# Moving the first weight transfer of a two-layer transformer kernel to ScalarE's queue, merging three early transfers and cutting the last output scaling into four pieces

## The chip, the cores and the metric

The kernel runs on one core of a Trainium2 chip. A core has TensorE (PE, the matmul engine, with its weight loads listed as PEld), VectorE (DVE), ScalarE (ACT), GpSimd (POOL) and SyncE (SP, which here only issues DMA transfers), and 16 DMA engines. The metric is the device time of one execution in microseconds; lower is better. Durations and start times below come from one profiled execution, counted from the start of its span.

## The reference

The reference is a two-layer hybrid block over 16 meta tokens and 256 input tokens of width 1024. Cut to what matters here:

```
h = concat(meta, x)
for li in range(2):
    h = h + mixer(rms_norm(h, norm_mix_g[li]), w_in[li], ...)      # retention, HGRN2, differential attention
    h = h + conv_ffn(rms_norm(h, norm_ffn_g[li]), w_ffn_in[li], ...)
out = rms_norm(h, norm_final_g)[:, PAD:]                           # 256 x 1024
```

with rms_norm(x, g) = x * rsqrt(mean(x*x) + 1e-6) * g. All weights are float32, and most of the time goes into the products with them.

## The kernel before, in words

**Weights.** All weight matrices are laid out on the host as one stream of 128x128 tiles in the order of use, in chunks of eight tiles (`CHUNK_TILES`, 128x1024 float32, 512 KB). `_Weights.next` (class at L554) does for each chunk what a float32 product needs when it is made of three fast products: a DMA brings the chunk to `wraw`, ACT rounds it to `whi`, DVE computes the remainder `wlo = wraw - whi`. There are three `wraw` buffers and four each of `whi` and `wlo`. Chunks 0 and 1 are brought and split in two halves of four tiles, all others whole.

**Products.** `products` (L862 to L864) issues three matmuls for each weight tile: `whi` with the rounded activations `xh`, `whi` with their remainder `xl`, `wlo` with `xh`. Activations lie as features by tokens: 128 partitions by 272 tokens, eight feature tiles k.

**The start.** x (with the meta tokens) lies in `h`, eight feature tiles, brought in four transfers of two tiles. `Norm.take` makes `xh` (ACT) and `xl` (DVE) of a tile k. The first norm is handled in a late way: the products start from x scaled by the gain alone, and the factor 1/rms (`rstd`) is multiplied into the products. For `rstd`, ACT squares pairs of tiles (`sum`, then `two_c` three times), POOL adds them, DVE folds the two halves, PE sums over partitions with a ones matrix (`ms`), and ACT takes Ln and Exp. After the fourth pair of output columns (`DEFER`), x is scaled by `rstd` itself: POOL makes `y`, ACT and DVE make a new `xh` and `xl` of it, for eight k. The first two output groups (`hq` 0 and 1) run interleaved over k = 0 to 3, so that chunk 0 holds the tiles of k = 0 (its first half) and k = 1, chunk 1 those of k = 2 and 3. Chunk 2 holds k = 4 to 7 of the first group, chunk 3 those of the second. Then come `hf` 0 to 3, two chunks each; `hf` 2 is the first that reads the scaled x.

**What sets the order.** The program is recorded as a list of operations with an engine, an estimated cost and a key, the due time (`plan.key`); `_Plan.order` (L407) plays this list through with the costs and picks, whenever an engine is free, the operation that can start first, by key among equals. `issue` (L508) emits the instructions in that order, and each engine runs its own in that order. In it a DMA issued by SP is taken as complete 2.0 us after its cost, others at once.

**The end.** `final` (L1340) computes the last products with tokens on partitions, two blocks of 128 tokens by two halves of 512 columns, and then for each block: ACT squares and sums, DVE multiplies the first half by the final gain, ACT takes Ln and Exp for the factor `dm`, then DVE scales the second half (L1390, from PSUM, with gain) and ACT the first half (L1391), and SP and ACT issue one output transfer of 256 KB each.

Nearly every instruction other than the matmuls is recorded through one helper, so its line is L549 in the profile; instructions are told apart by tile names.

## Time and profile before

| What | Value |
|---|---|
| Runs | 1330.01, 1329.83 and 1330.66 us; median 1330.01 |
| Profiled execution | 1330.22 us, span 1328.4 us, granted clock 0.999 |
| PE busy | 1317.2 us (99%), 11862 matmuls |
| DVE busy | 962.0 us (72%) |
| ACT busy | 813.3 us (61%) |
| POOL busy | 83.6 us (6%) |
| DMA | 219.07 MB, mean 165 GB/s |
| PE waits named in the trace | xl 2.8 us (3 times), ones_d 1.0 us, wlo 0.6 us |

The profiled execution is 1.8 us longer than its span and 0.2 us above the median of the runs. A busy share of PE of 99% does not mean that PE runs at its peak everywhere: matmuls overlap, and a matmul's row begins where it begins and may hold a wait. In a stream without waits, matmuls of 272 columns begin 0.125 us after one another.

### The profile page before, as it was taken

To read this page: it belongs to the slowest core of one execution; us is meant where nothing else is said; L and a number is where in the kernel's file an instruction comes from. 1 tells how busy PE (TensorE), PEld (TensorE's weight loads), DVE (VectorE), ACT (ScalarE), POOL (GpSimd) and SP (SyncE) were. 2 spreads that over 40 slices of the span, in tenths; PEclk is the share of its full clock that TensorE was granted. 3 is DMA by queue.
4 is the path that set the end of the run, shared out by engine and by line. 5 is a ranking of instruction groups with operands and counts; after the bars stand their busy time and mean duration, and the time that the engine had idled before them with its cause. 6 is when DMAs were issued, how large, how long until landed. Compare 5 with 4: busy or idle time off the path is not lost.

```text
span 1328.4 us, 28916 instructions
## 1 busy us (share of the span) xinstructions
PE 1317.2 (99%) x11862; PEld 1288.8 (97%) x11862; DVE 962.0 (72%) x1630; ACT 813.3 (61%) x1372; POOL 83.6 (6%) x161
## 2 busy tenths in 40 slices
PE   9999999999999999999999999999999999999998
PEld 9999999999999999999999999999999999999986
DVE  7575777697576689886564757776985867898753
ACT  6747454746676567665446474557565775766643
POOL 5000000001010020000030000000011100200000
PEclk9999999999999999999999999999999999999999
DMA  7644543443544545555555445444445445465653
GB/s 270 193 142 153 167 161 128 143 143 128 179 139 159 175 159 175 182 170 187 177 173 179 158 157 163 160 136 144 141 153 175 141 160 198 138 208 189 199 184 109
DMA packets 60755, 219.07 MB, mean 165 GB/s; under 512 B 6864, under 2 KB 6992, under 8 KB 60624
## 3 DMA queue, kind: packets, MB, share of 16 engines
q1 hardware_dynamic: 60336, 216.71, 49.6%
q8 instruction: 93, 1.52, 0.5%
q10 hardware_dynamic: 288, 0.52, 0.1%
q14 instruction: 38, 0.31, 0.1%
HBM read 216.16 MB, written 1.05 MB: 164 GB/s over the span
## 4 chain that ended last, share of the span: by engine, by line
PE 94%; DVE 4%; issue 1%; ACT 0%; DMA 0%; SPq 0%; DVEq 0%
PE main L862 27%; PE main L864 27%; PE main L863 26%; PE fo L1372 2%; PE fo L1374 2%; PE fo L1373 2%; PE lev L1053 1%; DVE two_b L549 1%; PE ds L1237 1%; DVE wlo L549 1%; PE ms L549 1%; PE do L549 1%; PE ro L549 1%; PE ho L549 1%; PE vt L549 1%
## 5 line engine op out<-in xcount | busy, mean ns | idle before, releaser
L862 PE MATMUL main<-xh,whi 128*128 128x272 f32 (+1 forms) x2368 | 693.4, 293 | 0.3 <-issue 0.3
L864 PE MATMUL main<-xh,wlo 128*128 128x272 f32 (+1 forms) x2368 | 680.4, 287 | 0.7 <-DVE wlo L549 0.6
L863 PE MATMUL main<-xl,whi 128*128 128x272 f32 (+1 forms) x2368 | 671.7, 284 | 2.8 <-DVE xl L549 2.8
L549 DVE TENSOR_TENSOR wlo<-wraw,whi 128x1024 fp32r<-128x1024 f32 (+1 forms) x408 | 496.8, 1223 | 201.2 <-ACT whi L549 200.3
L549 ACT ACTIVATE whi<-wraw 128x1024 fp32r<-128x1024 f32 (+1 forms) x408 | 426.5, 1048 | 231.5 <-PE main L863 166.1
L863 PEld LDWEIGHTS main<-xl,whi 128*128 128x128 f32 x2368 | 448.9, 190 | 4.0 <-DVE xl L549 3.4
L862 PEld LDWEIGHTS main<-xh,whi 128*128 128x128 f32 x2368 | 445.6, 188 | 2.1 <-issue 0.4
L864 PEld LDWEIGHTS main<-xh,wlo 128*128 128x128 f32 x2368 | 444.6, 188 | 2.0 <-DVE wlo L549 2.0
L549 DVE SCALAR_TENSOR_TENSOR two_b<-main,small,two_b 128x256 f32<-128x256 f32 (+2 forms) x144 | 65.4, 487 | 29.1 <-ACT two_b L549 27.4
L549 ACT ACTIVATE two_b<-main,small 128x272 f32<-128x272 f32 (+1 forms) x72 | 37.3, 566 | 28.7 <-PE main L864 28.7
L549 POOL TENSOR_TENSOR y<-h,rstd 128x272 f32<-128x272 f32 x32 | 34.8, 1121 | 316.4 <-ACT rstd L549 316.4
L864 PE MATMUL main<-ghi,wlo 128*128 128x272 f32 x176 | 51.0, 290 | 0.0
L862 PE MATMUL main<-ghi,whi 128*128 128x272 f32 x176 | 50.9, 289 | 0.0
L863 PE MATMUL main<-glo,whi 128*128 128x272 f32 x176 | 50.2, 285 | 0.0
L549 ACT ACTIVATE vsrc<-main 128x544 f32<-128x544 f32 x24 | 15.0, 626 | 39.4 <-PE main L864 39.2
L862 PE MATMUL main<-b0hi,whi 128*128 128x272 f32 (+1 forms) x128 | 38.2, 298 | 0.0
L862 PE MATMUL main<-b1hi,whi 128*128 128x272 f32 (+1 forms) x128 | 38.1, 298 | 0.0
L864 PE MATMUL main<-yhi,wlo 128*128 128x272 f32 (+1 forms) x128 | 36.7, 286 | 0.0
L864 PE MATMUL main<-b2hi,wlo 128*128 128x272 f32 (+1 forms) x128 | 36.6, 286 | 0.0
L864 PE MATMUL main<-b1hi,wlo 128*128 128x272 f32 (+1 forms) x128 | 36.6, 286 | 0.0
L864 PE MATMUL main<-b0hi,wlo 128*128 128x272 f32 (+1 forms) x128 | 36.6, 286 | 0.0
L862 PE MATMUL main<-yhi,whi 128*128 128x272 f32 (+1 forms) x128 | 36.5, 285 | 0.0
(244 smaller groups left out, 1933.0 us busy)
## 6 DMA issues: line engine op xcount, KB each, us to landing
wraw<-in_w SPq DMA_DIRECT2D x402, 512.0 KB, 3.4
h<-in_h SPq DMA_DIRECT2D x4, 272.0 KB, 5.6
dec<-in_dec SPq DMA_DIRECT2D x2, 544.0 KB, 5.3
wraw<-in_w SPq DMA_DIRECT2D x4, 256.0 KB, 4.9
const<-in_const SPq DMA_DIRECT2D x1, 937.0 KB, 5.9
gain<-in_gl SPq DMA_DIRECT2D x1, 512.0 KB, 5.2
out<-y ACTq DMA_DIRECT2D x2, 256.0 KB, 2.8
out<-y SPq DMA_DIRECT2D x2, 256.0 KB, 2.7
```

What stands on the lines that cost most here:

```text
L549: self.plan.add(self.name, lambda: f(*args, **kw), cost, outs, ins, args[2] if method == "activation" else None)
L862: nc.tensor.matmul(o, wh, hi, start=first, stop=False)
L863: nc.tensor.matmul(o, wh, lo, start=False, stop=False)
L864: nc.tensor.matmul(o, wl, hi, start=False, stop=last)
L1053: nc.tensor.matmul(o, keys, x, start=True, stop=True)
L1237: nc.tensor.matmul(ss[m][:, at : at + nk], q[half, hd, q0 : q0 + P], k[half, hd, :nk], start=True, stop=True)
L1372: nc.tensor.matmul(o, gh, wh, start=False, stop=False)
L1373: nc.tensor.matmul(o, gl, wh, start=False, stop=False)
L1374: nc.tensor.matmul(o, gh, wl, start=False, stop=end)
```

## The change

There are six edits.

1. The first half of chunk 0 is brought by ACT's DMA queue instead of SP's, with key -9.6, so that it is ACT's first instruction. The table load, which was ACT's first, is put ahead of the first activation, behind this transfer.
2. The second half of chunk 0 stays on SP's queue; chunk 1 is brought whole, while both chunks are still split into whi and wlo by halves.
3. x comes in three transfers instead of four: tiles 0-1, 2-3, and 4-7 in one.
4. The keys of `take` go from 1.4k - 4.0 to 1.4k - 6.5, and the rounding of a small constant (`ones_h`) is queued behind the xl of k = 1.
5. The planner's costs: the lag of a DMA is now held with the operation, 2.0 us for SP and 2.0 us plus the time for its bytes for other queues; an issue on ACT's queue costs 0.42 us instead of 0.06 us.
6. For the last group of `final`, the scaling is made in four pieces of 256 columns: ACT the first, DVE the third, POOL the second, DVE the fourth, with four transfers of 128 KB, on ACT's, SP's, SP's and ACT's queue.

On each engine the instructions are in the order of before from about chunk 12 on, up to the last group. In the first 40 us these rows differ. ACT before and after (`whi0a` is the first half of chunk 0, `xh4` is k = 4, `sq` the squares in the order of pairs, `fh` and `fl` the xh and xl of the scaled x):

```
before: table, ones_h, xh0, xh1, whi0a, sq0, whi0b, xh2, xh3, whi1a, sq1, whi1b, xh4, xh5, whi2, xh6, xh7, sq2, whi3, whi4, sq3, hq, whi5, rstd, whi6, ...
after:  DMA w0a, table, whi0a, xh0, xh1, whi0b, xh2, xh3, ones_h, sq0, whi1a, whi1b, sq1, xh4, xh5, xh6, xh7, whi2, sq2, whi3, whi4, sq3, hq, whi5, whi6, rstd, ...
```

and DVE:

```
before: xl0, xl1, wlo0a, wlo0b, xl2, xl3, wlo1a, wlo1b, xl4, xl5, wlo2, xl6, xl7, wlo3, wlo4, sum, wlo5, hq, ...,
        wlo9, fl4, fl5, fl6, hf1, fl7, wlo10, wlo11, masks
after:  wlo0a, xl0, xl1, wlo0b, xl2, xl3, wlo1a, wlo1b, xl4, xl5, xl6, xl7, wlo2, wlo3, wlo4, sum, wlo5, wlo6, hq, ...,
        wlo9, (parameters), fl4, fl5, masks, hf1, wlo10, fl6, fl7, wlo11
```

SP's queue begins with small, h0-1, w0b, h2-3, w1, h4-7, w2, w3, w4, w5, w6 (before: small, h0-1, w0a, w0b, h2-3, w1a, w1b, h4-5, w2, h6-7, w3, w4, w5, a second part of small, w6). On PE only the matmul `ms` moves, two tiles forward, into chunk 3.

The diff:

```
--- before.py
+++ after.py
@@ -302,11 +302,11 @@
 
 
 class _Op:
-    __slots__ = ("engine", "run", "cost", "key", "func", "tiles", "need", "after", "ready")
+    __slots__ = ("engine", "run", "cost", "key", "func", "tiles", "need", "after", "ready", "lag")
 
     def __init__(self, engine, run, cost, key, func):
         self.engine, self.run, self.cost, self.key, self.func = engine, run, cost, key, func
-        self.tiles, self.need, self.after, self.ready = set(), 0, [], 0.0
+        self.tiles, self.need, self.after, self.ready, self.lag = set(), 0, [], 0.0, 0.0
 
 
 class _Plan:
@@ -489,7 +489,7 @@
                     f.remove(min(f))
             engines[e] = t + cost
             self.busy[e] += cost
-            done = t + cost + (2.0 if e == "sp" else 0.0)
+            done = t + cost + op.lag
             for n in op.tiles:
                 left[n] -= 1
                 if left[n] == 0:
@@ -506,7 +506,9 @@
         return out
 
     def issue(self):
-        order = [None] + self.order()
+        order = self.order()
+
+        order.insert(next(i for i, op in enumerate(order) if op is not None and op.func is not None), None)
         with self.tc.manual_schedule():
             for op in order:
                 if op is None:
@@ -546,7 +548,10 @@
                 cost = max(0.214 if args[1].shape[-1] > 32 else 0.07, 4 * n / 2400)
             elif method == "dma_start":
                 cost = self.fixed + self.each * n * outs[0].shape[0]
-            self.plan.add(self.name, lambda: f(*args, **kw), cost, outs, ins, args[2] if method == "activation" else None)
+            op = self.plan.add(self.name, lambda: f(*args, **kw), cost, outs, ins, args[2] if method == "activation" else None)
+            if method == "dma_start":
+
+                op.lag = 2.0 if self.name == "sp" else 2.0 + 4 / 360e3 * n * outs[0].shape[0]
 
         return call
 
@@ -555,9 +560,9 @@
 
 
 
-    def __init__(self, plan, pool, w, act, dve, sp):
+    def __init__(self, plan, pool, w, act, dve, sp, first):
         self.plan, self.pool, self.w = plan, pool, w
-        self.act, self.dve, self.sp = act, dve, sp
+        self.act, self.dve, self.sp, self.first = act, dve, sp, first
         self.used = 0
         self.places = _places()
 
@@ -575,13 +580,19 @@
             hi = self.plan.tile(self.pool, room, F32R, "whi", 4, f"whi{c}")
             lo = self.plan.tile(self.pool, room, F32R, "wlo", 4, f"wlo{c}")
             self.plan.key = due - LEAD
-            pieces = 1 if c > 1 else 2
-            for p in range(pieces):
-                n = CHUNK_TILES // pieces
-                cols = slice(p * n * P, (p + 1) * n * P)
-                self.sp.dma_start(raw[:, cols], self.w[c][:, cols])
-                for first, at, step, runs, each in _runs(self.places[c][p * n : (p + 1) * n]):
-                    src = raw[:, (p * n + first) * P : (p * n + first + runs * each) * P].rearrange("p (r x) -> p r x", r=runs)
+
+            half = CHUNK_TILES // 2
+            for first in range(0, CHUNK_TILES, half if c == 0 else CHUNK_TILES):
+                cols = slice(first * P, (first + half if c == 0 else CHUNK_TILES) * P)
+                queue = self.sp
+                if (c, first) == (0, 0):
+                    queue, self.plan.key = self.first, -9.6
+                queue.dma_start(raw[:, cols], self.w[c][:, cols])
+                self.plan.key = due - LEAD
+            n = half if c < 2 else CHUNK_TILES
+            for a in range(0, CHUNK_TILES, n):
+                for first, at, step, runs, each in _runs(self.places[c][a : a + n]):
+                    src = raw[:, (a + first) * P : (a + first + runs * each) * P].rearrange("p (r x) -> p r x", r=runs)
                     self.act.activation(self.part(hi, at, step, runs, each), src, AF.Copy)
                     self.dve.tensor_tensor(out=self.part(lo, at, step, runs, each), in0=src, in1=self.part(hi, at, step, runs, each).bitcast(F32), op=SUB)
             self.plan.key = due
@@ -612,7 +623,7 @@
     pe = _Engine(plan, nc.tensor, "pe", 0.0, 4 / 2400)
     pool = _Engine(plan, nc.gpsimd, "pool", 0.04, 0.85e-3)
     sync = _Engine(plan, nc.sync, "sp", 0.06, 4 / 360e3)
-    act_queue = _Engine(plan, nc.scalar, "act", 0.06, 0.0)
+    act_queue = _Engine(plan, nc.scalar, "act", 0.42, 0.0)
 
     cp = ctx.enter_context(tc.tile_pool(name="cp", bufs=1))
     wp = ctx.enter_context(tc.tile_pool(name="wp", bufs=3))
@@ -622,7 +633,7 @@
     mp = ctx.enter_context(tc.tile_pool(name="mp", bufs=2, space=PSUM))
     bp = ctx.enter_context(tc.tile_pool(name="bp", bufs=2, space=PSUM))
 
-    weights = _Weights(plan, wp, a["w"], act, dve, sync)
+    weights = _Weights(plan, wp, a["w"], act, dve, sync, act_queue)
     serial = [0]
 
     def new(pool_, shape, dt, tag, bufs, name):
@@ -675,9 +686,9 @@
     plan.key = -10.0
     sync.dma_start(small[:, :S_LB], a["small"][:, :S_LB])
     h = fixed([P, KD, T], "h")
-    for k in range(0, KD, 2):
+    for k, n in ((0, 2), (2, 2), (4, 4)):
         plan.key = -9.0 if k == 0 else 1.4 * k - 7.0
-        sync.dma_start(h[:, k : k + 2, :].rearrange("p a t -> p (a t)"), a["h"][:, k * T : (k + 2) * T])
+        sync.dma_start(h[:, k : k + n, :].rearrange("p a t -> p (a t)"), a["h"][:, k * T : (k + n) * T])
     plan.key = 7.0 + EARLY
     sync.dma_start(small[:, S_LB:], a["small"][:, S_LB:])
     plan.key = 12.0 + EARLY
@@ -713,6 +724,7 @@
         pe.matmul(warm[:, :P], ones_d, ones_d, start=True, stop=True)
     plan.key = -5.0
     ones_h = ones_round(1.0 / 128, "ones_h")
+    rounded = plan.ops[-1]
     eps = fixed([P, 1], "eps")
     pool.memset(eps, EPS)
     fmap = fixed([P, DEPTH], "fmap")
@@ -943,8 +955,10 @@
         if li == 0:
             norm = Norm(small[:, S_GM : S_GM + KD], adds=pool)
             for k in range(KD):
-                plan.key = 1.4 * k - 4.0
+                plan.key = 1.4 * k - 6.5
                 norm.take([k])
+                if k == 1:
+                    plan.queue(rounded, plan.ops[-1])
             for j in range(4):
                 plan.key = 1.0 + 2.5 * j
                 norm.square([2 * j, 2 * j + 1])
@@ -1387,11 +1401,24 @@
                     continue
                 act.activation(ms[3], ms[1], AF.Ln, scale=1.0 / D, bias=ms[2])
                 act.activation(ms[3], ms[3], AF.Exp, scale=-0.5)
-                stt(y[:, t, cols], o, ms[3], gain[:, cols], MUL, MUL)
-                act.activation(y[:, t, :BANK], y[:, t, :BANK], AF.Copy, scale=ms[3])
-                for c, queue in ((1, sync), (0, act_queue)):
-                    cols = slice(c * BANK, (c + 1) * BANK)
-                    queue.dma_start(a["out"][:, t * D + c * BANK : t * D + (c + 1) * BANK], y[:, t, cols])
+
+                def part(first, n, queue, engine):
+                    yt = y[:, t, first : first + n]
+                    if engine is dve:
+                        stt(yt, o[:, first - BANK : first - BANK + n], ms[3], gain[:, first : first + n], MUL, MUL)
+                    elif engine is act:
+                        act.activation(yt, yt, AF.Copy, scale=ms[3])
+                    else:
+                        pool.tensor_scalar(out=yt, in0=yt, scalar1=ms[3], scalar2=None, op0=MUL)
+                    queue.dma_start(a["out"][:, t * D + first : t * D + first + n], yt)
+
+                if (t, c) == groups[-1]:
+                    for i, x in enumerate(((0, BANK // 2, act_queue, act), (BANK, BANK // 2, sync, dve), (BANK // 2, BANK // 2, sync, pool), (BANK + BANK // 2, BANK // 2, act_queue, dve))):
+                        plan.key = clock[0] + 0.1 * i
+                        part(*x)
+                else:
+                    part(BANK, BANK, sync, dve)
+                    part(0, BANK, act_queue, act)
 
         for name, j in ORDER:
             if name == "+ret":
```

## The prediction

> **What bounds the kernel now.** I read the page first, for the shares and the chain that ended last, then the timeline of the first 40 us and of the last 6, where the change lies.
>
> ```profile
> span 1328.4 us, 28916 instructions
> PE 1317.2 (99%) x11862; PEld 1288.8 (97%) x11862; DVE 962.0 (72%) x1630; ACT 813.3 (61%) x1372; POOL 83.6 (6%) x161
> ...
> PE 94%; DVE 4%; issue 1%; ACT 0%; DMA 0%; SPq 0%; DVEq 0%
> ```
>
> PE sets the time: 94% of the last chain is its own. Outside the first 40 us and the end the order on every engine is unchanged, so what the change can move is the start (the wait before PE's first product, and PE's gaps there) and the tail behind PE's last product. 0.2% of this kernel, about what a measurement can tell from no change, is 2.66 us.
>
> ```profile
> 0.73 1.28 ACT L513 ACT_TABLE_LOAD   x1 [0.73 <-PEq L1561]
> ...
> 1.18 0.42 SPq L549 DMA_DIRECT2D h<-in_h  x1
> 1.65 0.90 SPq L549 DMA_DIRECT2D wraw<-in_w  x2
> ...
> 4.02 0.94 ACT L549 ACTIVATE xh<-h,small 128x272 fp32r<-128x272 f32 x2 [1.69 <-DMA h<-in_h]
> ...
> 5.06 0.63 ACT L549 ACTIVATE whi<-wraw 128x512 fp32r<-128x512 f32 x1
> ...
> 6.47 0.39 PE L864 MATMUL main<-xh,wlo 128*128 128x272 f32 x1 [0.21 <-DVE wlo L549]
> ...
> 7.93 0.93 ACT L549 ACTIVATE xh<-h,small 128x272 fp32r<-128x272 f32 x2 [0.91 <-DMA h<-in_h]
> ...
> 10.16 0.39 PE L864 MATMUL main<-xh,wlo 128*128 128x272 f32 x1 [0.21 <-DVE wlo L549]
> ...
> 10.48 1.43 DVE L549 TENSOR_TENSOR wlo<-wraw,whi 128x512 fp32r<-128x512 f32 x1 [0.37 <-ACT whi L549]
> ...
> 12.66 1.21 DVE L549 TENSOR_TENSOR wlo<-wraw,whi 128x1024 fp32r<-128x1024 f32 x1
> ...
> 13.93 0.39 PE L864 MATMUL main<-xh,wlo 128*128 128x272 f32 x1 [0.21 <-DVE wlo L549]
> ```
>
> The first product starts at 5.75 and PE then stops at the third (6.47), at 9.44 and 10.16 (chunk 1, k = 2), at 11.97 (k = 3) and at 13.93 (chunk 2): against the pitch of 0.125 us these starts and the slow one behind each lose 2.2 us by 16 us. All wait for ACT's and DVE's splitting. From the chain of waits:
>
> ```profile
> 34.85 1.13 DVE wlo L549
> 35.98 0.42 DVE xl L549
> 36.45 0.39 PE main L863
> ```
>
> PE stops once more, 35.24 to 36.45 (1.06 us lost), for the first xl of the scaled x with k = 4 (`fl4`). So the most that the start can give is 2.2 + 1.06 + about 1 us of earlier begin, 4.3 us.
>
> ```profile
> 1322.94 0.53 ACT L549 ACTIVATE dm<-dm 128x1 f32<-128x1 f32 x2
> 1323.51 0.72 ACT L549 ACTIVATE y<-y,dm 128x512 f32<-128x512 f32 x1
> 1323.51 0.75 DVE L549 SCALAR_TENSOR_TENSOR y<-fo,dm,gain 128x512 f32<-128x512 f32 x1 [1.46 <-ACT dm L549]
> 1324.26 0.36 ACTq L549 DMA_DIRECT2D out<-y  x1
> ```
>
> The tail: 6.4 us from PE's last product to the end, of which scaling takes 0.75, a transfer 2.7 to 2.8 from issue to landing, closing about 1.3.
>
> **The start, step by step.** I give each instruction the later of its engine's last end and its inputs' ends, with these rows: xh 0.51 us (0.43 to the next), xl 0.49 (0.41), whi of a half 0.63 (0.53), whole 1.05 (0.95), wlo of a half 0.69 (0.60), whole 1.21 (1.14), squares 0.64. The same walk over the kernel before gives 13.87 for 13.93 and 36.91 for 36.45, so it runs 0.46 late by then; this is taken off below.
>
> *First weights.* ACT issues its transfer at 0.73 instead of SP's 1.65. The table load moves back by an issue (0.36 to 0.41), to 2.4; it is hidden, as ACT waits for data until 4.02 anyway. The shortest h transfer landed 2.8 us after issue: 3.5 for w0a, 3.7 with x's first tiles beside it. x landed at 3.98; sharing delays it by between nothing and 0.7 (the 0.67 that eight packets of 84 ns take); I take 4.25. whi0a 3.75 to 4.36, wlo0a 4.40 to 5.08, xh0 4.29 to 4.80, xl0 5.00 to 5.49, PE's second product 5.54, its third 5.67: 0.8 us ahead of 6.47. If w0a gained nothing, whi0a would still go ahead of xh0, 0 to 0.4 later than now.
>
> *k = 2.* Fewer bytes stand before h2-3 (1.08 MB, not 1.34); at the 250 GB/s of the first 16 us that is 1 us, so it lands at 6.7 instead of 7.9 (bounds 6.2 and 7.9). ACT then has xh2, xh3, ones_h (0.31, moved here from 2.03 where it cost nothing), the squares and whi1a: 6.75 + 2 x 0.43 + 0.25 + 0.55 = 8.4 to 9.0. The whole w1 lands at about 8.2 (cumulative bytes as before: w1a and w1b by 9.1), no later than ACT is ready; if it comes at 9.0, all below is 0.65 later. wlo1a ends at 9.73, PE goes on at 9.78: 0.38 ahead.
>
> *k = 3.* whi1b follows whi1a, wlo1b ends at 10.33; the stop at 11.97 (0.3) goes. Lead 0.7.
>
> *Chunk 2: here the lead is lost.* x's last four tiles land at once, at about 9.8 (11.8 for the last before), and the new order puts four xh ahead of whi2 and four xl ahead of wlo2; before, two of each stood behind. ACT: 10.0 + 4 x 0.43 = 11.7, whi2 to 12.74. DVE: the first xl meets POOL's sum. The row at 10.48 shows what that costs: a wlo of 0.69 took 1.43 beside POOL's 1.36. xl4 starts at 11.40, four xl end at 13.13, wlo2 goes 13.05 to 14.27, and PE's first wlo of chunk 2 is at 14.32 instead of 13.93: 0.4 behind. With the 0.15 that PE loses before at 15.45 for xl6 and xl7, 0.25 behind.
>
> *The norm.* The second sum (1.36) and wlo3 come 14.2 to 16.6, the third sum ends at 17.8, DVE's fold at 19.2, `ms` at 19.9. But rstd now stands behind whi6 on ACT, and w6 is issued when wlo3 frees its buffer (16.6) and lands 3.4 later (the median), 20.0; whi6 ends at 21.04, rstd at 22.06 against 21.55. Behind it wait POOL's eight y.
>
> *The scaled x.* The parameters' first half moves ahead of wlo7, which frees ACT for whi9 earlier; fl4 comes at 35.3, and PE, arriving at 35.8, no longer stops there: 1.06 gained. Late next: fl6. DVE now runs masks (0.32), hf1 (0.71) and wlo10 (1.21) ahead of it: 36.12 + 0.3 + 0.65 + 1.13 = 38.20, done 38.70, where PE wants k = 6 at 37.3. It goes on at 38.75; before, the same product was at 38.06. That is 0.69 late, less the walk's 0.46: **0.2 us slower**. The sum is small because four gains (0.8, 0.3, 0.15, 1.06) end in DVE's queue, which is busy 22.0 of the 24 us from 16 to 40.
>
> Everything from the second landing on shifts one for one with h2-3 and w1, so the landing bounds (0.5 early, 1.2 late) are the start's: -0.3 to +1.4; without the 0.69 of fl6 (if wlo10 falls early) -0.9.
>
> **The tail.** ACT and DVE make 256 columns in 0.51 and 0.48 (0.72 and 0.75 less 256 times the slopes, 0.21 and 0.27), so the first two transfers are issued at 1324.04 instead of 1324.26 and 1324.28; DVE's second piece ends at 1324.40, ACT issues it at 1324.43. POOL has no row for a scaling of 256 columns: bounds 0.31 (memset of 256) and 1.06 (256/272 of y's mean of 1.12, contended); nearest is the copy of 128 columns, 0.36, which with its slope gives 0.56, and SP's first issue hides it until 1324.4. At 1.06 its transfer is issued 0.2 later. The four pieces start 0.22 earlier but are finer, and a packet of half the size takes more than half the time (1280 bytes 55 ns, 2048 bytes 84: 9% more over the 1.5 us of data). Gain 0.1; bounds 0.5 gained and 0.15 lost, the latter from two more landings for SP to await.
> The Trainium skill (DMA: Bandwidth & Descriptors, Anatomy of one DMA) puts about 2.0 us of fixed cost on each transfer plus bytes over 436 GB/s; by that, as an estimate, a 128 KB piece issued 0.15 later lands 0.15 earlier. The rows give 2.7 to 2.8 for 256 KB, near its 2.6.
>
> **Sum.** +0.2 - 0.1 = +0.1 us. The profiled execution is 1330.22 and stands 0.2 above the median; so 1330.1 for the runs.
>
> **Rivals.**
> *The lead is kept, faster.* If x's last tiles land before POOL's first sum, the xl pass before it, and wlo2 is not late; PE keeps 0.7 and the stop at 36.45 goes (1.06): 0.7 + 1.06 and 0.1 to 0.5 of tail, 1.9 to 2.3, 1328.0; with fl6 still late, 0.9, 1329.1. For it: both stops are real. Against: DVE's row of 8 xl, four half wlo and wlo2 takes 8 x 0.41 + 4 x 0.6 + 1.2 = 6.9 us without any stop, and the walk has only 2.3 us of stops between 4.4 and 14.3.
> *POOL's second sum gets in before wlo2, slower.* Then wlo2 waits 1.15 and PE stands until 15.5; `ms` and rstd follow late: 1331.4. It decides by whether the squares end (13.3) before the fourth xl (13.1): 0.2 us apart.
> The Trainium skill (SBUF — State Buffer, Who interferes with whom) says that the first of the two to start holds the shared port for a whole instruction and the other is blocked; the row at 10.48 agrees with it.
> *ACT's queue brings w0a no earlier*, because both queues share the engines, which are busy over 90% from 3.2 us on: then the start is 0.4 later than taken and the time 1330.5. Against: nothing moves before 1.6 us.
>
> **How the numbers follow.** Forecast 0.55 (1329.3 to 1330.9), lead kept 0.22, POOL first 0.13, no earlier weights 0.10. Faster than 1327.35 needs all of the first rival and its largest tail: 0.08 with what I don't see; slower than 1332.67 needs the POOL case and late landings: 0.06; within 0.2%: 0.86. The range goes from the middle of the first rival, 1328.5, to the second's end, 1331.6.
>
> **What would show it.** Right: ACT's transfer at about 0.73, PE's third product near 5.7, the stop at 11.97 gone, wlo2 near 13.1 to 14.3 with PE waiting for it, no stop at fl4 but one at fl6 near 38, four output transfers. Wrong: whi0a not before 4.9, wlo2 before 13.0, rstd before 21, or PE's chain changed after 60 us.

## The result, and the profile after

The changed kernel takes 1332.86 us (median, 1330.85 to 1336.56), the kernel before beside it 1330.01 (1329.74 to 1330.79): a ratio of 1.0021, 95% interval 1.0014 to 1.0029. It is 0.2% slower, about the size that a measurement of this kernel can tell, and the time lies above the range predicted (1328.5 to 1331.6, forecast 1330.1).

The page of the changed kernel, its span, the engines' busy times and the chain that ended last:

```profile
span 1331.1 us, 28916 instructions
PE 1316.9 (99%) x11862; PEld 1288.3 (97%) x11862; DVE 963.2 (72%) x1631; ACT 813.2 (61%) x1372; POOL 82.7 (6%) x162
...
PE 93%; DVE 4%; issue 1%; DMA 1%; ACT 1%; SPq 0%; POOLq 0%; ACTq 0%; DVEq 0%
```

PE is busy no longer than before (1316.9 for 1317.2 us), and the profiled execution is 2.6 us longer (1332.86 for 1330.22). So the loss is PE standing still. The view of waits of the changed kernel (who waited, for whom: total, times, longest) names three places:

```profile
PE main L875 <- DVE xl L551: 3.1, 3, 1.5
PE main L876 <- DVE wlo L551: 1.2, 2, 1.0
...
PE lev L1067 <- issue: 1.1, 1, 1.1
```

The first two are in the first 40 us. The third, a wait for nothing that the profile shows ("issue"), is new at this place; the kernel before has one such wait near 190 us. The timeline of the changed kernel (start, duration, engine; in brackets the idle time before and who ended it) gives the start:

```profile
0.71 0.41 ACTq L551 DMA_DIRECT2D wraw<-in_w  x1
1.15 1.28 ACT L515 ACT_TABLE_LOAD   x1 [1.15 <-PEq L1588]
4.33 0.63 ACT L551 ACTIVATE whi<-wraw 128x512 fp32r<-128x512 f32 x1 [1.89 <-DMA wraw<-in_w]
5.08 0.94 ACT L551 ACTIVATE xh<-h,small 128x272 fp32r<-128x272 f32 x2
...
7.81 0.94 ACT L551 ACTIVATE xh<-h,small 128x272 fp32r<-128x272 f32 x2 [0.78 <-DMA h<-in_h]
...
10.07 0.39 PE L874 MATMUL main<-xh,whi 128*128 128x272 f32 x1 [0.76 <-ACT whi L551]
...
15.30 0.39 PE L876 MATMUL main<-xh,wlo 128*128 128x272 f32 x1 [1.03 <-DVE wlo L551]
...
22.64 0.43 ACT L551 ACTIVATE rstd<-rstd 128x272 f32<-128x272 f32 x1
...
36.27 0.91 DVE L551 SCALAR_TENSOR_TENSOR xl<-y,small,xh 128x272 fp32r<-128x272 f32 x2
37.09 0.32 DVE L551 CAST masks<-levf 128x320 uint8<-128x320 f32 x1
37.33 0.72 DVE L551 TENSOR_TENSOR hf<-main,rstd 128x544 f32<-128x544 f32 x1
37.96 1.22 DVE L551 TENSOR_TENSOR wlo<-wraw,whi 128x1024 fp32r<-128x1024 f32 x1
39.09 0.91 DVE L551 SCALAR_TENSOR_TENSOR xl<-y,small,xh 128x272 fp32r<-128x272 f32 x2
...
39.65 0.39 PE L875 MATMUL main<-xl,whi 128*128 128x272 f32 x1 [1.07 <-DVE xl L551]
```

ACT's transfer goes first, but its data are rounded at 4.33, and x's third and fourth tile at 7.81, hardly earlier than before (7.93). Chunk 2's low part is 1.37 us late (15.30 for 13.93). At fl4, its first product with the xl of the scaled x of k = 4, PE is 0.37 late (36.82 for 36.45) and hardly waits: the lateness has used up the stop that the kernel before has there. At fl6, the same for k = 6, it is 1.60 late (39.65 for 38.05), behind masks, hf1 and chunk 10 on DVE. In the kernel before the xl of k = 6 stands ahead of hf1, the third of the three in the first of these rows:

```profile
35.90 1.32 DVE L549 SCALAR_TENSOR_TENSOR xl<-y,small,xh 128x272 fp32r<-128x272 f32 x3
37.14 0.71 DVE L549 TENSOR_TENSOR hf<-main,rstd 128x544 f32<-128x544 f32 x1
...
38.05 0.28 PE L863 MATMUL main<-xl,whi 128*128 128x272 f32 x1
```

Behind the stop the next product is slow too, and PE is 1.70 late. After that its lateness changes twice. It falls by 0.36 near 190 us, where the kernel before stops by "issue" (two products begin 0.46 us apart there). It rises by 1.22 at 858 us, in a burst of 64 small matmuls of layer 2. The burst of the kernel before, from its timeline, and behind it that of the changed one:

```profile
855.41 0.74 PE L1053 MATMUL lev<-hq,hf 128*32 128x16 f32 x64
```

```profile
856.75 0.46 PE L1067 MATMUL lev<-hq,hf 128*32 128x16 f32 x33
858.26 0.44 PE L1067 MATMUL lev<-hq,hf 128*32 128x16 f32 x31 [1.06 <-issue]
```

1.70 - 0.36 + 1.22 = 2.56, and PE's last product is 2.57 late. The tail adds 0.1:

```profile
1326.08 0.88 DVE L551 SCALAR_TENSOR_TENSOR y<-fo,dm,gain 128x256 f32<-128x256 f32 x2 [1.50 <-ACT dm L551]
1326.08 0.51 ACT L551 ACTIVATE y<-y,dm 128x256 f32<-128x256 f32 x1
1326.14 0.93 POOL L551 TENSOR_SCALAR y<-y,dm 128x256 f32<-128x256 f32 x1 [175.11 <-ACT dm L551]
1326.59 0.84 SPq L551 DMA_DIRECT2D out<-y  x2
1326.61 0.84 ACTq L551 DMA_DIRECT2D out<-y  x2
```

The first two transfers go 0.2 us earlier behind `dm` than before, but POOL's piece takes 0.93, so the last of the four is issued only at 1327.10.

### The profile page after: what moved, and what is told of

It is laid out like the page before. It is cut to its first block, busy times and chain, and to the rows that moved or that the text cites. A ratio compares the mean times of both kernels' runs of the same rounds, so it can differ in the third digit from the quotient of the medians.

```text
span 1331.1 us, 28916 instructions
## 1 busy us (share of the span) xinstructions
PE 1316.9 (99%) x11862; PEld 1288.3 (97%) x11862; DVE 963.2 (72%) x1631; ACT 813.2 (61%) x1372; POOL 82.7 (6%) x162
## 4 chain that ended last, share of the span: by engine, by line
PE 93%; DVE 4%; issue 1%; DMA 1%; ACT 1%; SPq 0%; POOLq 0%; ACTq 0%; DVEq 0%
PE main L874 27%; PE main L876 27%; PE main L875 26%; PE fo L1388 1%; PE fo L1386 1%; PE fo L1387 1%; PE lev L1067 1%; DVE wlo L551 1%; DVE two_b L551 1%; PE ds L1251 1%; PE do L551 1%; DVE xl L551 1%; PE ms L551 1%; PE ro L551 1%; PE ho L551 1%
```

## The experiments

In the table the last four columns say how late PE is: how much later than in the profiled execution of the kernel before it starts the same product, at fl4, at fl6, ahead of layer 2's burst (840 to 858 us), and at its last one. Medians, ratios and intervals are against the kernel before, run on the same chip in the same series (1330.17 to 1330.42).

| Kernel | median us | ratio (95%) | fl4 | fl6 | ahead of burst | last |
|---|---|---|---|---|---|---|
| a_again | 1332.39 | 1.0017 (1.0008 to 1.0026) | +0.03 | +1.26 | +1.16 | +2.38 |
| tail_only | 1329.72 | 0.9997 (0.9989 to 1.0006) | -0.27 | -0.28 | -0.13 | -1.39 |
| head_only | 1332.00 | 1.0017 (1.0008 to 1.0026) | +0.59 | +1.82 | +2.31 | +3.53 |
| w0a_sp | 1332.80 | 1.0020 (1.0011 to 1.0029) | -0.14 | +1.08 | +1.06 | +1.94 |
| shift_after | 1332.39 | 1.0014 (1.0005 to 1.0023) | +0.18 | +1.39 | +1.14 | +1.13 |
| shift_before | 1332.87 | 1.0017 (1.0008 to 1.0026) | +1.47 | +2.13 | +2.63 | +2.63 |
| fix_fl6 | 1330.79 | 1.0001 (0.9992 to 1.0009) | +0.90 | +0.97 | +0.67 | +0.66 |
| fix_all | 1332.23 | 1.0014 (1.0005 to 1.0023) | +1.31 | +1.38 | +1.94 | +1.95 |
| dve_plus | 1330.95 | 1.0005 (0.9996 to 1.0014) | -0.11 | +1.11 | +0.95 | +0.82 |
| dve_minus | 1330.56 | 1.0003 (0.9994 to 1.0012) | -0.44 | -0.45 | +0.06 | +0.06 |
| x67_first | 1330.62 | 1.0003 (0.9995 to 1.0012) | +0.09 | +0.09 | +0.08 | +0.19 |
| best_a | 1330.28 | 1.0000 (0.9991 to 1.0009) | -0.91 | -1.02 | +0.30 | +0.30 |
| both_minus | 1333.62 | 1.0025 (1.0014 to 1.0035) | +0.91 | +1.38 | +2.09 | +2.94 |
| rstd_first | 1332.75 | 1.0020 (1.0011 to 1.0029) | +0.64 | +1.87 | +2.04 | +2.15 |
| best_b | 1331.52 | 1.0009 (1.0000 to 1.0018) | +1.11 | +1.01 | +0.87 | +0.88 |
| best_c | 1329.10 | 0.9991 (0.9983 to 1.0000) | -1.65 | -1.76 | -1.90 | -1.01 |
| dec_after | 1332.08 | 1.0011 (1.0002 to 1.0020) | -0.19 | +1.04 | +0.81 | +0.93 |
| dec_best | 1328.67 | 0.9988 (0.9979 to 0.9997) | -1.42 | -1.53 | -1.67 | -1.66 |

The same start comes out up to 0.8 us apart from one execution to the next: the changed kernel, a_again, head_only, shift_after, dve_plus and dec_after have the same order there and are 1.04 to 1.82 late at fl6. So a difference of less than 0.8 us at fl6 between two executions says little. Within one execution the same six agree: from fl4 to fl6 each gets 1.21 to 1.23 later.

### Which part costs: start or tail

`a_again` is the changed kernel unaltered. `tail_only` is the kernel before with the changed tail, `head_only` the changed kernel with the old tail:

```
tail_only:  before.py with `def part ... part(0, BANK, act_queue, act)` of the change in `final`
head_only:  after.py  with `stt(...)`, `act.activation(...)` and the two whole transfers of before in `final`
```

> The changed kernel once more, unaltered, for a second profile. Theory 1, the order of the splitting work at the start costs it (wlo of chunk 2 behind four xl, wlo of chunk 10 ahead of the scaled xl of k = 6): PE's product on k = 6 of chunk 9 is again about 1.6 us later than the 38.05 of before, and the stop of 1.24 us at lev in the second layer (a wait for nothing that the trace names) is chance and may be gone. Theory 2, ACT's queue beside SP's makes the first landings late and scattered: the landings of the first weights and of x move by 0.3 us or more between the two profiles. Theory 3, PE's own instruction loading: the stop without a releaser is there again, at this or another place. Time 1331 to 1334 by all three.

> The kernel before with the last scaling in four pieces and nothing else changed. Theory 1 and 2: the start is that of before, and the tail from the last square to the end goes from 6.2 to 6.3 us as in the changed kernel's profile; 1330.1, same as before within 0.2 us. Rival, the tail is what costs and scatters: 1331 or more.

> The changed kernel with the last scaling in two halves as before; the start is the changed one. Theory 1: PE 1.4 to 1.6 us late from chunk 9 on, 1331.5 to 1333. Theory 2 gives the same time with a wide scatter. The tail as the cause: 1330.0.

The start alone costs what the whole change costs (1332.00 and 1332.39), the tail nothing that can be told from no change (0.9997). Its profile has PE 1.39 us early at the end, but 1.26 of that gain comes between 1170 and 1260 us, where the programs are the same, by a slightly shorter pitch; it is no work of the tail.

### Is it ACT's queue?

`w0a_sp` is head_only with the first transfer on SP's queue, which then issues w0a at 0.74, small at 1.17, x's first tiles at 1.65; the order on all other engines is that of head_only.

```
-    weights = _Weights(plan, wp, a["w"], act, dve, sync, act_queue)
+    sync_first = _Engine(plan, nc.sync, "act", 0.42, 0.0)
+    weights = _Weights(plan, wp, a["w"], act, dve, sync, sync_first)
```

> As head_only, with the order of ACT, DVE, POOL and PE unaltered, but the first half of the first weights is issued by SP, behind its small first transfer and ahead of x, so that ACT's queue moves nothing at the start. Theory 1: the landings of x tiles 2-3 and of chunk 1 are those of head_only within 0.4 us and the time is as long, 1331.3 to 1333. Theory 2: x and chunk 1 land earlier, the scatter goes, and the time falls to 1330.5 or below.

PE's first product comes 0.7 us later than in head_only, and at fl6 and at the end nothing is left of that: 1332.80, no faster than head_only. x's third and fourth tile land at 7.18 us, in head_only at 7.24. The queue is not the cause.

### The stop at 858 us: first theory, TensorE's own code

The trace lists TensorE's code as transfers of 16 KB. The one read at 850.23 in the kernel before comes at 855.93 in the changed kernel, and in all four kernels with the new start PE stops behind it. TensorE's program has 177 separate waits there instead of 178, so its code is one instruction shorter.

```
shift_after (after.py):   -    ones_d = ones(1.0 / D, "ones_d")
                          +    ones_d = fixed([P, P], "ones_d")
                          +    pool.memset(ones_d[:, : P // 2], 1.0 / D)
                          +    dve.memset(ones_d[:, P // 2 :], 1.0 / D)
shift_before (before.py): in the planned order, whi of chunk 6 moved directly ahead of rstd (ACT)
```

> The changed kernel with the constant that the warm-up matmuls read written half by POOL and half by DVE, so that TensorE's first matmul waits for two engines and TensorE's program gets one instruction more, as in the kernel before (178 separate waits, not 177); nothing else moves. Theory A (the stop at 858 us comes from where the blocks of TensorE's code end): the block that was read at 855.9 us is read near 851 to 852 again, the stop of 1.24 us in the 64 lev matmuls is gone, PE's lateness at its end falls from 2.4 to 1.1 to 1.4 us, time 1331.0 to 1331.5; the start is unaltered (fl6's product 1.2 to 1.6 late). Rival B (the stop is a result of the data or of an engine that comes late in layer 2): it stays, PE ends 2.4 late, 1332.4.

> The kernel before with one step moved: on ACT chunk 6's high part ahead of the two steps of rstd, as the changed kernel has it. By this one of TensorE's separate waits goes (177). Theory A: the stop of about 1.2 us at 858 us appears in the old kernel too, and 0.5 to 1.2 us is lost at the scaled x because rstd starts at 22.2 instead of 20.6: 1331.4 to 1332.4. Rival B (the stop belongs to the new start alone): no stop; 1330.0 if POOL's and DVE's scaled x have that much slack, up to 1331.2 if not.

The first came out as theory A has it in its profiled execution (no stop, +1.13 at the end). The second speaks against it: 177 waits, and no stop. The theory fell. The timed runs of shift_after lie 1.0 us above its profiled execution (1331.40); whether the stop is there in some of them is open.

`shift_before` shows something else. With chunk 6's high part ahead of rstd, the old order loses 3.0 us at the scaled x (2.6 are left ahead of the burst, since its stop near 190 us is gone). From its timeline:

```profile
36.38 0.39 PE L889 MATMUL main<-xh,whi 128*128 128x272 f32 x1 [0.90 <-ACT xh L575]
...
37.92 0.39 PE L890 MATMUL main<-xl,whi 128*128 128x272 f32 x1 [1.14 <-DVE xl L575]
```

The old order had no slack for a later rstd.

### The stop at fl6: DVE's order

A step was added to `_Plan.issue` that moves single operations in the planned order; `ahead(ops, mark)` puts them directly ahead of another one, `behind` behind it.

```
fix_fl6 (after.py):   ahead(scaled xl k=6,7; masks)                                    # DVE
fix_all (after.py):   the same, and
                      ahead(whi1a; ones_h)                                             # ACT
                      ahead(whi2; xh6)   ahead(wlo2; xl6)                              # ACT, DVE
                      ahead(rstd; whi6)                                                # ACT
x67_first (after.py): ahead(scaled xl k=6,7; wlo10)   behind(masks, hf1; scaled xl k=7)  # DVE
```

In fix_fl6 and fix_all the move also puts the new x ahead of hf1's last reads of the old one, so hf1's products for k = 6 and 7 take the scaled x, and those tiles are not the reference's. x67_first has the same order on DVE without that.

> The changed kernel with the rounding of scaled x k = 6 and 7 on DVE ahead of the masks, hf1's evacuation and chunk 10's low part, nothing else. If these 1.9 us on DVE are what fl6 waits for: its product comes 0.3 to 0.5 late instead of 1.3 to 1.6, PE ends 1.0 to 1.2 earlier, the stop at 858 us stays, 1331.2 to 1331.6. If the lateness at fl6 only moves to hf1's evacuation (0.9 later, so its accumulator comes free later): 1332.0 to 1332.4.

> The changed kernel with four steps moved back: chunk 1's first high part ahead of ones_h and the first square (ACT), chunk 2's high and low parts ahead of x k = 6 and 7 (ACT, DVE), rstd ahead of chunk 6's high part (ACT), scaled x k = 6 and 7 ahead of the masks (DVE). TensorE's program has 178 separate waits by this. If order is all that the new start loses: k = 2's product near 9.4 us, chunk 2's low product near 14.2 to 14.4, fl6's product at most 38.1, no stop at 858, 1329.4 to 1330.2. If ACT's queue and the whole h4-7 cost by themselves (later landings): still 0.5 to 1.0 late at fl6, 1330.5 to 1331.2.

> The changed kernel with scaled x k = 6 and 7 on DVE ahead of the masks, hf1's evacuation and chunk 10's low part, as in fix_fl6, but hf1's last products read the unscaled x, as they must. If these 1.9 us on DVE are what fl6 waits for: its product comes 0.2 to 0.5 late against the kernel before instead of 1.3 to 1.6. DVE's program gets two separate waits more by the new order (as in fix_fl6), so by theory C the stop at 858 us goes too: 1330.4 to 1330.9. If hf1's evacuation (0.9 later) holds TensorE up instead: 1331.5 to 1332.4.

DVE and PE of x67_first, from its timeline:

```profile
35.98 1.73 DVE L581 SCALAR_TENSOR_TENSOR xl<-y,small,xh 128x272 fp32r<-128x272 f32 x4
37.64 0.32 DVE L581 CAST masks<-levf 128x320 uint8<-128x320 f32 x1
37.87 0.71 DVE L581 TENSOR_TENSOR hf<-main,rstd 128x544 f32<-128x544 f32 x1
...
38.14 0.28 PE L906 MATMUL main<-xl,whi 128*128 128x272 f32 x1
```

fl6's product starts at 38.14 without a wait, +0.09, though chunk 2 was still 1.13 late in this execution; hf1's evacuation and chunk 10, now later, hold nobody up. So the order of three steps on DVE is the 1.2 us at fl6. With that mended, and no stop at 858 us in it either, the new start is as fast as the old one (1.0003), not faster: PE arrives at fl4 0.09 late instead of 1 us early, because the lateness of chunk 2 has used up the stop that was there. fix_all gained nothing by its four moves: it is 1.42 late behind fl6 and gets 0.52 more by a longer stop near 190 us. From the start of x's third tile on ACT (xh2) to chunk 2's first low product it takes 7.01 us, the changed kernel 7.49 and the kernel before 6.00. So putting chunk 2's parts ahead of x again takes back a third of what the new start loses there. ACT now waits until 8.97 for chunk 1, which lands whole at 8.95; in the kernel before its first half landed at 8.56. No run separates what the merged transfers cost from the rest.

`rstd_first` moves rstd alone:

```
rstd_first (after.py): ahead(rstd; whi6)       # ACT
```

> The changed kernel with the two steps of rstd ahead of chunk 6's high part on ACT, as in the kernel before; by it TensorE has 178 separate waits again. rstd starts near 21.0 instead of 22.1, POOL's y near 22.0 instead of 23.15. If fl6 waits for DVE's order (masks, hf1's evacuation and chunk 10's low part ahead of x k = 6 and 7): its product stays 1.0 to 1.4 late. If it waits for rstd over POOL: 0.3 or less. If the pair of counts (177 and 1337) makes the stop at 858 us, it goes here: PE ends 1.0 to 1.4 late, 1331.2; if 1337 on DVE alone makes it in the new start, it stays: 2.2 to 2.5 late, 1332.3.

rstd ends at 21.64 instead of 22.5 to 23.1, and fl6 stays 1.87 late: in the new order DVE sets fl6, not rstd. The stop at 858 us is gone in it, with 1336 DVE instructions ahead of the sum spoken of below and 178 separate waits on TensorE.

### The stop at 858 us: second theory, VectorE's code

Of the kernels run so far, those with the stop had 1337 DVE instructions (separate waits counted) ahead of layer 2's first sum, those without it 1338 or 1339, and with 1337 an 8 KB block of the other engines' code is read right behind one of TensorE's.

```
dve_plus (after.py):    +    extra = fixed([P, 1], "extra")
                        +    dve.memset(extra, 0.0)
dve_minus (before.py):  -            ts(subg[:, one], small[...], 1.0 - lambda_init(li), None, MUL)
                        +            pool.tensor_scalar(out=subg[:, one], in0=small[...], scalar1=1.0 - lambda_init(li), scalar2=None, op0=MUL)
both_minus (before.py): dve_minus, and whi6 moved ahead of rstd as in shift_before
```

> The changed kernel with one instruction more on DVE, a memset of one column that nothing reads, at its start; TensorE's program is unaltered (177 separate waits). Theory C (VectorE's code: the kernels with the stop have 1337 DVE instructions ahead of layer 2's first sum near 842 us, those without 1338 or 1339; with 1337 a block of 8 KB of the other engines' code is read 3 us later, 0.3 to 0.6 us behind the start of one of TensorE's blocks, and TensorE's next block comes 3 to 5 us late): the 8 KB block is read near 842.4, TensorE's next one near 851 to 852, no stop in the lev matmuls near 858, PE ends 1.1 to 1.4 late instead of 2.4, about 1331.2. Rival A (TensorE's own code is one instruction short): the stop stays, PE ends 2.4 late, 1332.4.

> The kernel before with the two small steps that write subg (128x1 each) on POOL instead of DVE; nothing else. If DVE then has 1337 instructions ahead of layer 2's first sum, theory C expects the 8 KB block at 844 to 845 instead of 841.2, beside TensorE's block at 844.0, TensorE's next block near 854 instead of 850.2 and a stop of 0.9 to 1.24 us near 857 in the old kernel: PE's end 0.9 to 1.3 later, 1331.0 to 1331.5. Rival A (TensorE's own count, which is unaltered): no stop, 1330.0 to 1330.4. The two steps on POOL lie between its y steps and cost 0 to 0.3 us at fl4.

> The kernel before with chunk 6's high part ahead of rstd on ACT (as in shift_before: 177 separate waits on TensorE) and subg's two steps on POOL (as in dve_minus: 1337 DVE instructions ahead of layer 2's first sum). If the pair of counts decides: the stop of about 1.2 us near 860 comes, on top of shift_before's 2.6: PE ends 3.6 to 3.9 late, 1333.5 to 1334.2. If the stop belongs to the new start by something else: PE ends 2.4 to 2.8 late, 1332.5 to 1333.0.

With a memset that nobody reads the stop is gone in the profile, and the changed kernel runs in 1330.95 us, where a_again took 1332.39 in another series. Their intervals overlap (1.0005 with 0.9996 to 1.0014, and 1.0017 with 1.0008 to 1.0026), so the timed runs agree with a gain but don't prove one. But dve_minus has the 1337 instructions and the two blocks 0.3 us apart, and no stop; both_minus has it (0.9 us; it ends 2.94 late and not 3.6 to 3.9, since it came to the burst 2.1 late and not 2.6); and best_c, below, has it with the blocks 3 us apart. This theory fell too. What it leaves: in the profiled executions one instruction on DVE, far from the place, goes with a stop of 1 us on PE.

### The parameters' small steps, and a faster kernel

In the kernel before, fl4 waits for the xl that stands behind 2.6 us of small steps on DVE, and for chunk 9's high part, which stands behind their Exp on ACT.

```
best_a (before.py + changed tail): behind(p, nlam, subg, fmap, lbp, keep, floor and both Exp; scaled xl k=7)
best_c (before.py + changed tail): behind(the same; wlo10)
best_b (after.py): rstd_first, x67_first, and behind(p, nlam, fmap, lbp, keep, floor of the second half; wlo10)
```

> The kernel before with the four-piece scaling of the last tile, and with the 16 small steps on the parameters (p, nlam, subg, fmap, lbp, keep, floor on DVE, the two Exp on ACT) behind the last scaled x instead of ahead of chunk 9's parts. In the kernel before they hold DVE from 32.2 to 34.8 and, over the Exp in ACT's queue, chunk 9's high part to 33.4. If they are what fl4's stop of 0.96 us waits for: no stop at 36.45, fl6 0.9 early, PE ends 0.9 to 1.0 early, and with 0.1 of the tail 1328.8 to 1329.2. If fl6 or the release of an accumulator takes the stop over: 1329.5 to 1330.0. If keep and floor come late for the gates: 1330.0 or more.

> The changed kernel with rstd ahead of chunk 6's high part (ACT) and, on DVE, scaled x k = 4 to 7, the masks, hf1's evacuation and chunk 10's low part ahead of the small steps on the parameters. If fl4 and fl6 wait for DVE's order alone: no stop at either, TensorE keeps the 0.9 to 1.3 it is late at chunk 2 and has won 0.96 at fl4: PE ends 0.0 to 0.4 late, 1329.9 to 1330.4 with the tail. If a stop takes their place (an accumulator, chunk 11): 1330.5 to 1331.2.

> best_a with the small steps on the parameters behind chunk 10's low part too, which they made 1.1 us late there. If nothing else takes the stop over: no stop at 36.45 nor at 39.62, PE ends 0.7 to 1.0 early, 1329.0 to 1329.5. If chunk 11's low part or the gates (keep, floor) do: 1329.8 to 1330.3.

best_a took the stop at fl4 away (-0.91) and got it back at chunk 10's low part, which now stood behind the small steps; DVE and PE from its timeline:

```profile
38.35 2.36 DVE L585 TENSOR_TENSOR wlo<-wraw,whi 128x1024 fp32r<-128x1024 f32 x2
...
39.62 0.39 PE L901 MATMUL main<-xh,wlo 128*128 128x272 f32 x1 [0.82 <-DVE wlo L585]
```

best_c puts them one chunk further back, and no stop takes its place: PE is 1.76 early at fl6 (0.7 of it is an early start of this execution, -0.72 at chunk 2) and 1.90 ahead of the burst. There it loses 0.91:

```profile
35.41 1.21 DVE L585 TENSOR_TENSOR wlo<-wraw,whi 128x1024 fp32r<-128x1024 f32 x1
36.55 0.15 DVE L585 TENSOR_TENSOR p<-small 128x8 f32<-128x8 f32 x1
...
853.51 0.45 PE L1090 MATMUL lev<-hq,hf 128*32 128x16 f32 x32
854.69 0.44 PE L1090 MATMUL lev<-hq,hf 128*32 128x16 f32 x32 [0.73 <-issue]
```

best_b has all of it on the new start. PE then stops at 34.59 for chunk 8's low part, which stands on DVE behind four xl and hf0's evacuation, reaches fl4 1.11 late and ends 0.88 late; 0.36 of that is this execution's start (chunk 2's first low product 1.49 late, in x67_first 1.13). It gains nothing over x67_first (ratios 1.0009 and 1.0003, with overlapping intervals).

### The stop at 858 us: third theory, the table's transfer

Once in each layer SP transfers the table `dec` (544 KB), 0.4 us after it issues a chunk of weights. From the records of transfers, in us (a gap is from the start of one matmul of the burst to the start of the next, the longest of the 64):

| Kernel | code block, and the next | dec's data | gap on PE in the burst |
|---|---|---|---|
| after | 845.40, 855.93 | 853.75 to 856.36 | 1.24 |
| a_again | 845.16, 855.75 | 854.10 to 856.42 | 1.24 |
| head_only | 846.23, 857.08 | 855.04 to 857.31 | 1.24 |
| w0a_sp | 845.07, 855.31 | 853.88 to 856.15 | 0.90 |
| both_minus | 846.12, 856.39 | 854.70 to 856.73 | 0.90 |
| best_c | 842.04, 852.29 | 850.48 to 852.97 | 0.91 |
| before | 844.01, 850.23 | 852.36 to 855.45 | 0.03 (none) |
| dve_plus | 844.89, 851.51 | 853.37 to 855.51 | 0.03 (none) |
| dve_minus | 844.00, 851.46 | 853.01 to 855.47 | 0.03 (none) |
| rstd_first | 846.37, 852.99 | 854.11 to 857.00 | 0.03 (none) |

In the six with the stop, the next block is read 10.2 to 10.9 us after the one before it, and its read begins 0.2 to 0.8 us before dec's data end. In the twelve without it (four of them shown) it is read 6.2 to 7.5 us after, 1.1 to 2.1 us ahead of dec's data. Among these eighteen nothing lies between.

That PE waits for this block itself is shown by when it goes on. In every execution with a stop in the burst, dec_after's of 0.14 us below included, the first matmul behind the stop starts 1.2 to 1.5 us after the read of the block has ended (in the changed kernel the read takes 0.88 us from 855.93, and PE goes on at 858.26). The stops near 190 us, in thirteen executions, end 1.2 to 1.6 us after the read of a block as well.

```
dec_after (after.py): behind(dec; the second chunk of weights after it)   # SP, in both layers
dec_best: best_c with the same
```

> The changed kernel with the transfer of the decay table dec (544 KB, once in each layer) issued by SP behind the next two chunks of weights instead of ahead of them; the programs of TensorE, VectorE, ScalarE and GpSimd are in the same order. dec is first read at 876.9 us in the changed kernel and lands at 856.7 there, so 8 to 10 us later costs nothing. Theory D (dec's transfer, on top of a chunk of weights, holds TensorE's code block back until it ends): the block read at 855.9 is read near 852, no stop at 858 us, perhaps a shorter one near 190 us too, PE ends 1.0 to 1.4 late, 1331.0 to 1331.4. If something else holds the block back (the chunks of weights themselves, the place in the code): the block at 855 to 856, the stop stays, 1332.4.

> best_c with dec behind the next two chunks of weights, as in dec_after. Theory D: the stop of 0.91 us at 854.7 goes, PE ends 1.7 to 2.0 early against the kernel before, 1328.1 to 1328.4, ratio 0.9985 to 0.999. If the stop stays or comes at another place: 1329.0 to 1329.3.

With dec out of the way the burst runs through in dec_best and has a gap of 0.14 us left in dec_after, which comes first:

```profile
856.22 0.86 PE L1099 MATMUL lev<-hq,hf 128*32 128x16 f32 x64
```

```profile
853.75 0.74 PE L1093 MATMUL lev<-hq,hf 128*32 128x16 f32 x64
```

In dec_best the block is read at 849.18, 6.8 us after the one before it, and PE keeps what the start gave: 1.67 early ahead of the burst, 1.66 at the end. At 1328.67 (0.9988, interval 0.9979 to 0.9997) it is the fastest kernel here, and the only one whose interval lies below 1; its difference from best_c (0.9991, 0.9983 to 1.0000) is within the noise. In dec_after the block still comes late (853.97, 9.2 us after the one before it, among two chunks of weights), 0.1 us too late: dec's transfer is not all that can hold it back. Its profiled execution takes 1331.24, its timed runs 1332.08, 0.3 below a_again: there the gain of a full microsecond is not shown. Nor does dec make the stop near 190 us: dec_best still has it (0.36 for 0.37 in best_c), though dec's data come at 196.5 there.

## Why the prediction was wrong

*The first weights.* Predicted: whi0a at 3.75, PE's third product at 5.67, 0.8 ahead. Measured: 4.33, and 6.42 (0.05 ahead; 6.17 to 6.86 over the executions with this start, 6.41 to 6.84 with the old one). The step failed. With a second queue at work the small first transfer took 1.85 us of data instead of 0.40 and the data of x's first tiles ended at 4.5 instead of 3.6. That is the third rival's mechanism, with a larger price than it was given; and it cost nothing in the end, as w0a_sp shows from the other side.

*k = 2, the landing of h2-3: the term of the sum that failed.* Predicted: h2-3 lands at 6.7 instead of 7.9, 1.2 us earlier, and xh2 starts at 6.75. Measured: it lands at 7.79 and xh2 starts at 7.81, before 7.90 and 7.93. Even that 0.1 is no gain: in the eight kernels with the old start it lands between 7.16 and 7.95 us (mean 7.58), in the eleven with the new one between 7.13 and 7.92 (mean 7.54). The gain put at 1.2 us is nothing that these runs can tell from zero. The count of bytes under it was wrong: in the order of the queues the same transfers stand ahead of h2-3 in both kernels (small, x's first two tiles and both halves of chunk 0, 1.07 MB with its own), with chunk 1 behind it, and 1.34 MB for the kernel before is half of chunk 1 too much. The edit moved only the issue, by 0.5 us (2.09 for 2.59). Why the landing didn't follow it stays open; between 4 and 10 us the DMA engines moved 335 GB/s before and 339 after.

Everything behind it was worked out well:

| | predicted | measured, from xh2's start, in after, a_again, dve_plus |
|---|---|---|
| wlo2's product behind xh2 | 14.32 - 6.75 = 7.57 | 7.49, 7.47, 7.48 |
| fl6's product behind xh2 | 38.75 - 6.75 = 32.00 | 31.84, 31.84, 31.79 |
| before: the same two | | 6.00 and 30.12 |

(Of the kernels whose order is the changed one up to fl6, head_only is the exception, with 32.61 at fl6.) So the new order is 1.5 us slower at chunk 2 and 1.7 at fl6 for a given landing, and a gain at the start needed h2-3 to land 1.7 us earlier. The prediction had it 1.2 earlier; it came no earlier.

*k = 3, chunk 2, norm.* The stop at 11.97 went, as predicted. At chunk 2 the new order lost what was predicted, and with the landing PE's first low product came at 15.30 instead of 14.32. rstd ended at 23.07 instead of 22.06, again the landing and no more.

*fl4 and fl6.* Right in kind: fl4's stop goes and fl6, behind masks, hf1 and wlo10, is late next; x67_first shows that these three steps are it. The size was wrong by the landing (xh2 1.06 later than predicted) and by a second error: the prediction took 0.46 off because the walk through the kernel before ended 0.46 late there. In the new order the walk was 0.16 late. Taken together, 38.29 was forecast and 39.65 measured.

*"Outside the first 40 us and the end the order on every engine is unchanged, so what the change can move is the start and the tail."* This failed, and a third of PE's lateness is from there: +1.22 at 858 us, less 0.36 near 190, of 2.57. The order was unchanged; the time at which blocks of code are read was not. The prediction named "PE's chain changed after 60 us" as a sign of its being wrong, with no price on it.

*The tail.* Forecast 0.1 gained, measured 0.1 lost in the profile and nothing in tail_only's timed runs; POOL's piece took 0.93, near the upper bound of 1.06 and not the 0.56 taken. The section of the Trainium skill that the prediction names there states its fit for transfers that GpSimd issues, and these are issued by SP and ACT; the four pieces of 128 KB landed 2.0 to 2.7 us after issue, around the 2.3 of that fit, and the last of them no earlier behind `dm` than the halves of before (3.6 us in both).

*The sum.* +0.1 was forecast and a slower kernel came out, but that the sign agrees is luck: the +0.1 is what is left of a gain that didn't come and of losses, one of which (the stop at 858 us) the prediction didn't see.

*The rivals.* The lead was not kept. POOL's second sum did not get in ahead of wlo2: that took its usual 1.22 us. The range was too narrow on the slow side: its bounds held the landing (+1.4 for the start) but nothing for the rest of the program.

What is shown: the start costs, not the tail; DVE's order makes fl6 late by 1.2 us; the stop at 858 us is a wait for a late block of code, comes and goes without any change of order near it, and in the two kernels in which dec is transferred later it is gone or 0.14 us long. What stays open: why the code block is held until dec's data end in some programs and gets in ahead of them in others, which of the start's edits costs what of the 1.5 us at chunk 2, how often the stop comes in executions without a profile (shift_after and dec_after ran 1.0 and 0.8 above their profiled execution), and what makes the block of code late near 190 us, where PE stops for 0 to 0.98 us.

## What to carry to other kernels

Before a start is reordered for an earlier first product, look for the step on the splitting engine that a later product waits for (here the xl of k = 6 on DVE, at 36 to 40 us), and ask of each moved step whether it now stands ahead of it; three steps cost 1.2 us there. Before a landing time is worked out from bytes, list the transfers that are issued ahead of it in both kernels: here they were the same, and the gain of 1.2 us was none. And when a kernel is bound by one engine's instruction stream, a change that leaves a place alone can still move it by 1 us, by when its code is read: compare the two traces product by product before a difference of 0.1% is put down to the edit.

## What the runs showed that was not expected

TensorE's code is read while it runs, in 93 blocks of 16 KB for 23,900 instructions. The Trainium skill (Runtime: NRT & Kernel Launch, Instruction fetch mechanics) says the same of the blocks and calls the cost of crossing one mostly hidden. Nearly all are hidden here too. Two are not in some of the programs: one near 190 us, and one near 855 us which, read 10.2 to 10.9 us after the one before it, at the end of a 544 KB transfer, stopped PE for 0.9 to 1.24 us in a burst of 64 matmuls that start about 9 ns apart.

A transfer on ACT's queue was no separate path. w0a's data took from 1.78 to 3.98 us, small's from 1.72 to 3.57 (before, alone, 1.74 to 2.14), and issuing w0a from SP instead changed the time by nothing that can be told (1332.80 and 1332.00). The Trainium skill (DMA: Bandwidth & Descriptors, Issuing engines are not separate DMA queues) has this rule: a second issuing engine saves the time of issuing, and the transfers share the same engines. The runs agree.
